# Splitting the normed mixer outputs where they are made, and passing them through DRAM as halves

## The chip, the cores and the metric

The kernel runs on one core of a Trainium2 chip. A core has five engines that run side by side, each with its own queue of instructions in a fixed order: TensorE (PE, matrix products), VectorE (DVE), ScalarE (ACT), GpSimd (POOL) and SyncE (SP, which here only issues DMA transfers). They share one on-chip memory (SBUF, 128 partitions) and the accumulators of TensorE (PSUM); DRAM is reached by DMA. The metric is the device time of one execution in microseconds.

## The reference

One layer of a decoder trunk over 2048 tokens of width 1024, in float32:

```python
proj = x @ w_in                       # q, k, v | b_gate, c_gate, h | p
mix  = concat(stick_breaking_attention(q, k, v),     # 8 heads x 64
              b_gate * conv3(c_gate * h),            # 4 groups x 64
              pooled(p) @ pool_w * pool_scale)       # 4 groups x 64
mix  = head_group_rmsnorm(mix, mix_norm_g)           # over each 64 columns
x = layer_norm(alpha * x + mix @ w_o, ln1_g, ln1_b)
x = layer_norm(alpha * x + relu(x @ w_up)**2 @ w_down, ln2_g, ln2_b)
```

## The kernel before

The tokens are cut into four chunks of 512. Products run on operands that are split into two halves: a tile t becomes hi = t rounded to the type that TensorE reads at full rate (fp32r), and lo = t - hi. A product of two such operands is then three products, hi by hi, hi by lo and lo by hi (lines 235 to 237 for the projections, 521 to 523 for the output). The helper `load` (line 177) makes the halves of what comes from DRAM: a DMA into a raw buffer (four buffers with the tag "raw", for all that is loaded this way), a cast on ScalarE (line 182), and a subtraction (line 184) on the engine that `low_engine` names: a counter of all such subtractions sends, from the fortieth on, every third to VectorE and the others to GpSimd.

The stages, by chunk pairs (0, 1) and (2, 3): projections of q, k and v, which go through DRAM already split; attention, which takes 224 of its 320 units in the second pair; the projections with convolution and pooling (`bchp`, groups 9, 7, 8 and 6 of the weights, for each pair); and the output stage (`out_stage`), which multiplies the normed mixer outputs by w_o, adds x, applies LayerNorm and sends the transposed rows on to the feed-forward part. From there on (classes `Up` and `down`) TensorE has products without a gap.

The order of instructions on each engine is set by a planner. It takes them by priority and by when a simulated machine could start them: blocks marked `early()` come first, attention (`PRIO`) second, and what bears no mark comes last, in the order of the program. So the unmarked projections, convolutions and output products fill in where attention leaves an engine free.

A mixer output of 128 columns of the concatenation (attention: the pair of heads j = 0 to 3; convolution j = 4, 5; pooling j = 6, 7) is normed by `rms` (line 281). A Square on ScalarE writes the tile `sq`. `rest` sums it by small products on TensorE, forms the inverse root (`rsqrt`, with a power on GpSimd), and spreads it into `sq` again. `scaled` transposes `sq` into PSUM and multiplies: `o = m * gain * ps` (line 302). Attention has one `sq` buffer and one `o` buffer ("a"). Convolution and pooling have one `sq` buffer for each of b0 and b1 and two buffers for `o`; the same buffers later hold LayerNorm's gain and bias (lines 559, 560). `sink` then does one thing: it stores `o` in DRAM, as `mscr[c][j]` (line 286).

`load_mix` (line 506) brings the eight outputs of a chunk back by `load`, at the highest priority, into the eight buffers of the tags "wh" and "wl". These are the buffers of the chunk before, and come free one by one as the last output product of that chunk reads them; the raw loads can run up to four tiles ahead. The last output of chunk 3 never leaves the chip: `last_mix` splits it in place of the store, on ScalarE and VectorE.

For chunk 0 the first products take four of its tiles first, and for chunk 3 seven of them (`ready`). The output product of a row block needs an accumulator in one of two PSUM buffers ("dn"), which line 554 on VectorE empties.

Of the kernel before, what the change touches and what calls it, by code (L numbers as in the profile page):

```python
# [10 lines left out]
F = mybir.dt.float32  # L11
R = mybir.dt.float32r
AF = mybir.ActivationFunctionType
ALU = mybir.AluOpType
# [3 lines left out]
P = 128  # L18
# [3 lines left out]
CH = 512  # L22
NC = S // CH
HEADS = 8
HD = 64
ND = D // P
# [17 lines left out]
def build(nc, tc, ctx, A, out):  # L44
    const = ctx.enter_context(tc.tile_pool(name="const", bufs=1))
    dram = ctx.enter_context(tc.tile_pool(name="dram", bufs=1, space=DRAM))

    nc.scalar.preload_act_table_set("sigmoid_and_others")
    ident = const.tile([P, P], F, name="ident")
    make_identity(nc, ident)  # L50
    eps_ln = const.tile([P, 1], F, name="eps_ln")
    nc.vector.memset(eps_ln, LN_EPS)

    qscr = [[dram.tile([2, HD, CH], F, name=f"qscr{c}_{h}") for h in range(HEADS)] for c in range(NC)]
    kscr = [[dram.tile([2, HD, CH], F, name=f"kscr{c}_{h}") for h in range(HEADS)] for c in range(NC)]
    vscr = [[dram.tile([4, P, 4, P], F, name=f"vscr{c}_{g}") for g in range(2)] for c in range(NC)]
    mscr = [[dram.tile([P, CH], F, name=f"mscr{c}_{j}") for j in range(ND)] for c in range(NC)]
    x1scr = [[dram.tile([P, D], F, name=f"x1scr{c}_{t}") for t in range(4)] for c in range(NC)]
    tscr = [[dram.tile([P, 2, 4, NQ, P], F, name=f"tscr{h}_{k}") for k in range(7)] for h in range(2)]
    hscr = [[[dram.tile([P, 4, CH], F, name=f"hscr{g}_{h}_{j}") for j in range(2)] for h in range(2)]  # L60
            for g in range(DFF // CH)]

    def split(dst_hi, dst_lo, src, scale=None):
        if scale is None:
            nc.scalar.copy(dst_hi, src)
            nc.vector.tensor_tensor(dst_lo, src, dst_hi.bitcast(F), ALU.subtract)  # L66
        else:
            nc.scalar.activation(dst_hi, src, AF.Identity, scale=scale)
            nc.vector.scalar_tensor_tensor(dst_lo, src, scale, dst_hi.bitcast(F), ALU.mult, ALU.subtract)

    expo = const.tile([P, 8], F, name="expo")
    nc.vector.memset(expo, -0.5)

    def rsqrt(pool, var, eps, shape, tag):

        v, s, t = (pool.tile(shape, F, name=f"{tag}{k}", tag=f"{tag}{k}", bufs=2) for k in "vst")
        nc.vector.tensor_scalar(v, var, eps, None, ALU.add)
        nc.gpsimd.tensor_tensor(s, v, expo[:, 0:shape[1]], ALU.pow)
        if shape[1] == 1:
            nc.vector.tensor_scalar(t, s, v, -0.5, ALU.mult, ALU.mult)  # L80
            nc.vector.tensor_scalar(t, t, s, 1.5, ALU.mult, ALU.add)
            nc.vector.tensor_scalar(s, s, t, None, ALU.mult)
            return s
        nc.vector.scalar_tensor_tensor(t, s, -0.5, v, ALU.mult, ALU.mult)
        nc.vector.scalar_tensor_tensor(t, t, 0.0, s, ALU.add, ALU.mult)
        nc.vector.scalar_tensor_tensor(s, t, 1.5, s, ALU.add, ALU.mult)
        return s

    def ln_stats(p, t, inverse):
        st = p.tile([P, 2, 6], F, name="st", tag="st", bufs=2)  # L90
        for i in range(2):
            nc.vector.bn_stats(st[:, i, :], t[:, i * 512:(i + 1) * 512])
        mv = p.tile([P, 2], F, name="mv", tag="mv", bufs=2)
        nc.vector.bn_aggr(mv, st)
        return mv[:, 0:1], inverse(p, mv[:, 1:2])

    def inverse_dve(p, var):
        return rsqrt(p, var, LN_EPS, [P, 1], "ln")

    def inverse_act(p, var):  # L100
        y, t = (p.tile([P, 1], F, name=f"ln{k}", tag=f"ln{k}", bufs=2) for k in "yt")
        nc.scalar.activation(y, var, AF.Ln, bias=eps_ln)
        nc.scalar.activation(y, y, AF.Exp, scale=-0.5)
        nc.scalar.activation(t, y, AF.Square)
        nc.vector.tensor_scalar(t, var, LN_EPS, t, ALU.add, ALU.mult)
        nc.vector.tensor_scalar(t, t, -0.5, 1.5, ALU.mult, ALU.add)
        nc.vector.tensor_scalar(y, y, t, None, ALU.mult)
        return y

    def layer_norm(p, t, g, b):  # L110
        m, y0 = ln_stats(p, t, inverse_dve)
        for i in range(2):
            h = t[:, i * 512:(i + 1) * 512]
            nc.vector.scalar_tensor_tensor(h, h, m, g[i], ALU.subtract, ALU.mult)
            nc.vector.scalar_tensor_tensor(h, h, y0, b[i], ALU.mult, ALU.add)

    def bcast(p, name):
        t = p.tile([P, D], F, name=name)
        nc.sync.dma_start(t, A[name].partition_broadcast(P))
        return t  # L120

    scr = qscr, kscr, vscr, mscr, x1scr, tscr
    with ExitStack() as up:
        pools = phase1(nc, tc, ctx, up, A, ident, scr, hscr, split, rsqrt, layer_norm, bcast)
    down(nc, tc, ctx, A, pools, hscr, x1scr, lambda p, t: ln_stats(p, t, inverse_act), bcast, out)


def phase1(nc, tc, whole, ctx, A, ident, scr, hscr, split, rsqrt, layer_norm, bcast):
    qscr, kscr, vscr, mscr, x1scr, tscr = scr
# [6 lines left out]
    pm = mixw.enter_context(tc.tile_pool(name="mixw", bufs=1, side="right", reuse_waits="tile"))  # L136
# [20 lines left out]
    for i in range(2):  # L157
        w = pd.tile([P, P], F, name=f"pw{i}")
# [18 lines left out]
    def load(src, name, shape, bufs):  # L177
        pool = px if name == "x" else pm
        raw = pd.tile(shape, F, name=f"{name}raw", tag="raw", bufs=RAW)
        nc.sync.dma_start(raw, src)  # L180
        h = pool.tile(shape, R, name=f"{name}h", tag=f"{name}h", bufs=bufs)
        nc.scalar.copy(h, raw)
        l = pool.tile(shape, R, name=f"{name}l", tag=f"{name}l", bufs=bufs)
        low_engine().tensor_tensor(l, raw, h.bitcast(F), ALU.subtract)
        return h, l
# [95 lines left out]
    def rms(m, j, c, ps_of, who):  # L281
        pool = p if who == "a" else pd
        sq = pool.tile([P, CH], F, name=f"sq{who}")
        nc.scalar.activation(sq, m, AF.Square)

        def rest(then, sink=lambda y: nc.sync.dma_start(mscr[c][j], y)):
            with early():
                var = ps_of()
                for t in range(4):
                    nc.tensor.matmul(var[:, 2 * t:2 * t + 2], sq[:, t * P:(t + 1) * P], blk, start=True, stop=True)  # L290
                y = rsqrt(pool, var[:, 0:8], RMS_EPS, [P, 8], f"rms{who[0]}")
                wide = sq.rearrange("p (g e) -> p g e", g=8)
                nc.scalar.activation(wide, y.unsqueeze(2).to_broadcast([P, 8, HD]), AF.Copy)

            def scaled():
                with early():
                    ps = ps_of()
                    for t in range(4):
                        ts = slice(t * P, (t + 1) * P)
                        nc.tensor.transpose(out=ps[:, ts], in_=sq[:, ts], identity=ident)  # L300
                    o = pool.tile([P, CH], F, name=f"o{who}", tag=f"rms{who[0]}y", bufs=len(who))
                    nc.vector.scalar_tensor_tensor(o, m, gain[:, j:j + 1], ps, ALU.mult, ALU.mult)
                    sink(o)
            then(scaled)
        return rest
# [190 lines left out]
    def halves(name, tags, bufs=1):  # L496
        t = []
        for i, tag in enumerate(tags):
            h = pd.tile([P, CH], F, name=f"{name}_{i}", tag=tag, bufs=bufs)
            nc.sync.dma_start(h, A[name][i * CH:(i + 1) * CH].partition_broadcast(P))  # L500
            t.append(h)
        return t

    mix = {}

    def load_mix(c, part):
        with early():
            mix.setdefault(c, []).extend(load(mscr[c][e], "w", [P, CH], ND) for e in part)

    def last_mix(y):  # L510
        h = pm.tile([P, CH], R, name="mh", tag="wh", bufs=ND)
# [157 lines left out]
class Up:  # L669
# [35 lines left out]
    def rest(self):  # L705
        self.pr = self.pool("upr")
        for i in (5, 6):
            self.load(0, i)
        pp = self.pt = self.whole.enter_context(self.tc.tile_pool(name="turnps", bufs=1, space=PSUM, side="right",
                                                                  reuse_waits="tile"))  # L710
        self.turn = Turn(self.nc, self.tc, self.pr, self.ident, self.tscr,
                         lambda: pp.tile([P, CH], F, name="tp", tag="tp", bufs=2),
                         {n: n for n in ("b0", "b1", "c0")} | {"x1h": "xs", "x1l": "xs"}, 3, nullcontext)
# [254 lines left out]
```

## Time and profile before

| | |
|---|---|
| median of 3 runs | 2456.9 us (2456.46 to 2458.3) |
| the profiled execution | 2459.65 us, span 2457.9 us |
| mean granted clock of TensorE | 0.994 |
| busy share of PE, DVE, ACT, POOL | 98%, 65%, 41%, 46% |
| instructions | 33072 |

The span is the time from the first to the last instruction of the profiled execution, which is what the rows below divide; its own time beside it includes what lies around the span. A busy share is an average over stages that differ. In views of windows each engine's column is its busy time in that stretch, PEclk the clock that TensorE was granted, as a share of full speed, and the DMA share the mean busy share of the 16 DMA engines.

### The profile page before, as it was taken

The page shows a single profiled execution, that of the slowest core. Times are in us where ns is not written, and L with a number is a line of the kernel's source. Part 1 is how long each engine was busy: PE and PEld are TensorE (multiplying, and loading weights), DVE is VectorE, ACT ScalarE, POOL GpSimd, SP SyncE. Part 2 cuts the span into 40 slices and gives each one's busy share as a digit, 9 for nine tenths or more (in the row PEclk, how much of TensorE's full clock was granted, in tenths as well). Part 3 has the DMA queues.
Part 4 walks back from the last instruction along what each step waited for, and adds up shares of the span by engine and source line. Part 5 has one row for each costly group of instructions (what it writes and reads, how often), then busy time and mean ns, then how long its engine had stood idle before and what let it go on. Part 6 is the DMA issues. An engine that isn't in the chain of part 4 may idle for free.

```text
span 2457.9 us, 33072 instructions
## 1 busy us (share of the span) xinstructions
PE 2398.0 (98%) x11728; PEld 1992.8 (81%) x11728; DVE 1589.8 (65%) x2227; ACT 1008.2 (41%) x1945; POOL 1136.3 (46%) x833
## 2 busy tenths in 40 slices
PE   8999999999999999999999999999999999999997
PEld 6988888778778787788888888888888888888886
DVE  3778777788987899976666656556316433333367
ACT  4667666655666656522333223222332101111123
POOL 2557555864775757634556545555201101101137
PEclk9999999999999999999999999999999999999999
DMA  8758645622422446557665383333525312212212
GB/s 239 193 148 235 174 138 148 195 78 91 158 82 95 141 149 220 201 216 289 221 225 192 112 333 125 116 103 112 173 75 172 110 53 86 86 49 78 80 60 112
DMA packets 164854, 360.37 MB, mean 147 GB/s; under 512 B 18640, under 2 KB 35024, under 8 KB 162896
## 3 DMA queue, kind: packets, MB, share of 16 engines
q1 hardware_dynamic: 164688, 358.25, 45.2%
q8 instruction: 93, 1.52, 0.3%
q14 instruction: 73, 0.60, 0.1%
HBM read 245.19 MB, written 112.98 MB: 146 GB/s over the span
## 4 chain that ended last, share of the span: by engine, by line
PE 78%; DVE 9%; DMA 4%; POOL 4%; issue 3%; ACT 2%; SPq 1%; DVEq 0%; ACTq 0%; POOLq 0%
PE dn L895 9%; PE dn L894 9%; PE dn L893 9%; PE b L792 7%; PE c L792 4%; PE a L792 4%; PE z L433 4%; PE dn L235 3%; PE dn L236 3%; PE b L795 3%; PE dn L237 3%; PE tp L465 3%; PE c L795 2%; PE a L795 2%; PE dn L521 2%
## 5 line engine op out<-in xcount | busy, mean ns | idle before, releaser
L448 POOL TENSOR_TENSOR g<-g,sig 128x512 f32<-128x512 f32 (+2 forms) x320 | 381.6, 1197 | 338.3 <-DVE g L446 144.4
L893 PE MATMUL dn<-d,ht 128*128 128x512 f32 x1024 | 398.3, 389 | 0.0
L894 PE MATMUL dn<-d,ht 128*128 128x512 f32 x1024 | 398.3, 389 | 0.0
L895 PE MATMUL dn<-d,ht 128*128 128x512 f32 x1024 | 397.7, 389 | 0.0
L732 POOL TENSOR_TENSOR w<-raw,w 128x512 fp32r<-128x512 f32 x186 | 253.9, 1371 | 240.9 <-ACT w L731 240.9
L899 DVE TENSOR_TENSOR y<-dn,y 128x512 f32<-128x512 f32 x224 | 154.2, 689 | 322.2 <-PE dn L895 322.1
L858 POOL TENSOR_TENSOR d<-draw,d 128x1024 fp32r<-128x1024 f32 x32 | 77.6, 2438 | 507.4 <-ACT d L857 507.2
L446 DVE TENSOR_TENSOR_SCAN g<-beta,g,z 128x513 f32<-128x513 f32 x192 | 244.1, 1275 | 48.5 <-ACT sig L438 46.3
L436 ACT ACTIVATE beta<-z 128x512 f32<-128x512 f32 (+2 forms) x320 | 172.9, 541 | 159.4 <-PE z L433 146.3
L871 ACT CAST ht<-draw 128x512 fp32r<-128x512 f32 x128 | 74.5, 620 | 380.3 <-PE dn L895 347.3
L895 PEld LDWEIGHTS dn<-d,ht 128*128 128x128 f32 x1024 | 192.2, 188 | 39.9
L893 PEld LDWEIGHTS dn<-d,ht 128*128 128x128 f32 x1024 | 192.2, 188 | 39.9
L894 PEld LDWEIGHTS dn<-d,ht 128*128 128x128 f32 x1024 | 192.2, 188 | 39.9
L731 ACT CAST w<-raw 128x512 fp32r<-128x512 f32 x186 | 114.1, 621 | 252.9 <-PE b L795 143.8
L235 PE MATMUL dn<-xh,wh 128*128 128x512 f32 x512 | 206.9, 407 | 10.3 <-DVE qk L66 5.3
L433 PE MATMUL z<-k,q 128*128 128x512 f32 (+3 forms) x640 | 192.6, 380 | 17.8 <-DVE g L446 12.7
L236 PE MATMUL dn<-xl,wh 128*128 128x512 f32 x512 | 206.8, 404 | 0.0
L237 PE MATMUL dn<-xh,wl 128*128 128x512 f32 x512 | 206.7, 404 | 0.0
L469 DVE TENSOR_TENSOR tl<-tp,th 128x512 fp32r<-128x512 f32 (+1 forms) x320 | 184.3, 596 | 30.3 <-ACT th L468 29.5
L465 PE MATMUL tp<-ident,g 128*128 128x128 f32 x1088 | 190.8, 274 | 1.9 <-DVE tl L469 0.8
L792 PE MATMUL b<-x,w 128*128 128x512 f32 x768 | 190.2, 390 | 2.1 <-ACT w L731 1.5
L468 ACT CAST th<-tp 128x512 fp32r<-128x512 f32 (+1 forms) x320 | 161.5, 535 | 63.9 <-PE tp L465 51.9
(195 smaller groups left out, 4983.9 us busy)
## 6 DMA issues: line engine op xcount, KB each, us to landing
hscr<-h SPq DMA_DIRECT2D x128, 256.0 KB, 2.8
draw<-hscr SPq DMA_DIRECT2D x64, 512.0 KB, 3.9
raw<-in_w_up SPq DMA_DIRECT2D x62, 512.0 KB, 4.4
x<-tscr SPq DMA_DIRECT2D x14, 2048.0 KB, 12.3
wraw<-in_w_in SPq DMA_DIRECT2D x80, 256.0 KB, 3.3
k<-kscr SPq DMA_DIRECT2D x80, 256.0 KB, 3.0
v<-vscr SPq DMA_DIRECT2D x80, 256.0 KB, 2.8
xraw<-in_xt SPq DMA_DIRECT2D x64, 256.0 KB, 3.1
```

The costliest lines, as they stand in the source:

```text
L235: nc.tensor.matmul(ps, wh, xh, start=(d == 0), stop=False)
L236: nc.tensor.matmul(ps, wh, xl, start=False, stop=False)
L237: nc.tensor.matmul(ps, wl, xh, start=False, stop=(d == ND - 1))
L433: nc.tensor.matmul(z[:, 0:w], q[:, b, j * P:(j + 1) * P], m["k"][:, 0:w], start=(b == 0), stop=(b == 1))
L446: nc.vector.tensor_tensor_scan(left, rev, idle, st["prev"][j][:, OFF - 1:OFF], ALU.mult, ALU.bypass)
L448: nc.gpsimd.tensor_tensor(gv, gv, sig[:, 0:w], ALU.mult)
L465: nc.tensor.transpose(out=tp[:, j * P:(j + 1) * P], in_=m["g"][j][:, cols], identity=ident)
L732: self.nc.gpsimd.tensor_tensor(w[:, 1], src, w.bitcast(F)[:, 0], ALU.subtract)
L792: nc.tensor.matmul(ps, wk[:, 0, d], x[:, i, :, d, :], start=(first and d == 0 and i == 0), stop=False, skip_group_check=True)
L893: nc.tensor.matmul(ps, hh[:, ts], dh[:, ds], start=(i == 0), stop=False)
L894: nc.tensor.matmul(ps, hh[:, ts], dl[:, ds], start=False, stop=False)
L895: nc.tensor.matmul(ps, hl[:, ts], dh[:, ds], start=False, stop=(i == 3))
```

## The change

The output `o` is split where it is made. The new function `halves` (not to be confused with the loader of the same name below it, line 496) casts `o` into the buffer of `sq`, which has been read by then, subtracts on GpSimd in place, and stores both tiles; the buffer in DRAM has room for the two. For convolution and pooling it runs outside the `early()` block, so with the priority of the program's unmarked parts; for attention with attention's own. The last output of chunk 3 keeps its way through `last_mix`. `load_mix` loads the two halves straight into "wh" and "wl", without a raw buffer, a cast or a subtraction.

```diff
-    mscr = [[dram.tile([P, CH], F, name=f"mscr{c}_{j}") for j in range(ND)] for c in range(NC)]
+    mscr = [[dram.tile([2, P, CH], F, name=f"mscr{c}_{j}") for j in range(ND)] for c in range(NC)]
...
-        def rest(then, sink=lambda y: nc.sync.dma_start(mscr[c][j], y)):
+        def halves(y):
+            hi, lo = sq.bitcast(R), y.bitcast(R)
+            nc.scalar.copy(hi, y)
+            nc.gpsimd.tensor_tensor(lo, y, sq, ALU.subtract)
+            nc.sync.dma_start(mscr[c][j][0], sq)
+            nc.sync.dma_start(mscr[c][j][1], y)
+
+        def rest(then, sink=halves):
...
                     nc.vector.scalar_tensor_tensor(o, m, gain[:, j:j + 1], ps, ALU.mult, ALU.mult)
+                    if sink is not halves:
+                        sink(o)
+                if sink is halves:
                     sink(o)
...
-            mix.setdefault(c, []).extend(load(mscr[c][e], "w", [P, CH], ND) for e in part)
+            for e in part:
+                t = [pm.tile([P, CH], F, name=f"w{n}", tag=f"w{n}", bufs=ND) for n in "hl"]
+                for i in range(2):
+                    nc.sync.dma_start(t[i], mscr[c][e][i])
+                mix.setdefault(c, []).append([a.bitcast(R) for a in t])
```

## Rows read from the trace of the kernel before

**Rows 1.** The page's first part: busy us (share of span) xinstructions, by engine.
```profile
PE 2398.0 (98%) x11728; PEld 1992.8 (81%) x11728; DVE 1589.8 (65%) x2227; ACT 1008.2 (41%) x1945; POOL 1136.3 (46%) x833
```
**Rows 2.** Windows: stretch, length, busy of PE, PEld, DVE, ACT, POOL, PEclk, DMA share, GB/s.
```profile
100.00:440.00 340.00, 336.77 (x2046) 294.89 (x2045) 261.98 (x359) 225.27 (x484) 192.93 (x162) 1.00 0.60 166
500.00:850.00 350.00, 334.33 (x1736) 269.89 (x1735) 295.78 (x408) 217.45 (x441) 230.96 (x179) 0.99 0.34 107
850.00:1130.00 280.00, 268.61 (x1335) 219.29 (x1333) 244.98 (x387) 132.04 (x259) 151.13 (x118) 0.99 0.57 196
...
1600.00:1650.00 50.00, 50.00 (x223) 41.39 (x222) 30.76 (x37) 14.05 (x24) 27.68 (x20) 1.00 0.35 114
```
**Rows 3.** The same view, two stretches of 10 us in the output stage.
```profile
850.00:860.00 10.00, 7.93 (x31) 6.15 (x29) 9.21 (x13) 8.46 (x17) 9.24 (x8) 0.83 0.63 201
940.00:950.00 10.00, 7.09 (x32) 5.36 (x33) 9.81 (x13) 8.50 (x17) 10.00 (x8) 1.00 0.74 240
```
**Rows 4.** Groups by line and form, 820 to 1140: count, busy us, mean ns, idle before.
```profile
L184 POOL TENSOR_TENSOR wl<-wraw,wh 128x512 fp32r<-128x512 f32 x21 | 30.1, 1443 | 6.1 <-PE dn L522 3.7 <-ACT wh L182 2.4
...
L182 ACT CAST wh<-wraw 128x512 fp32r<-128x512 f32 x31 | 18.6, 631 | 27.1 <-PE dn L522 16.5 <-DMA wraw<-mscr 10.2
...
L184 DVE TENSOR_TENSOR wl<-wraw,wh 128x512 fp32r<-128x512 f32 x10 | 10.8, 1077 | 4.6 <-ACT wh L182 4.1 <-PE dn L522 0.4
```
**Rows 5.** Timeline of PE: start, duration, instruction, [idle before it <-releaser].
```profile
853.32 1.22 PE L433 MATMUL z<-k,q 128*128 128x512 f32 x2 [2.07 <-DVE rmsbt L85]
...
941.22 0.73 PE L433 MATMUL z<-k,q 128*128 128x512 f32 x2 [1.27 <-DVE g L446]
...
946.01 0.50 PE L521 MATMUL dn<-xh,wh 128*128 128x512 f32 x1 [1.69 <-DVE r L554]
...
1031.52 0.65 PE L650 MATMUL dn<-ident,r 128*128 128x128 f32 x4 [1.28 <-DVE x1l L628]
```
**Rows 6.** Timeline of DVE, three subtractions of mixer tiles.
```profile
938.84 1.13 DVE L184 TENSOR_TENSOR wl<-wraw,wh 128x512 fp32r<-128x512 f32 x1
...
943.76 1.60 DVE L184 TENSOR_TENSOR wl<-wraw,wh 128x512 fp32r<-128x512 f32 x1
...
1029.01 0.67 DVE L184 TENSOR_TENSOR wl<-wraw,wh 128x512 fp32r<-128x512 f32 x1
```
**Rows 7.** The chain of waits from 845 to 853 us: start, us, what.
```profile
847.97 1.25 POOL wl L184
849.21 1.61 POOL rmsbs L78
```
**Rows 8.** Mixer buffer: stores (ns min/median/max, first to last), DMA median us to landing.
```profile
L286 SPq DMA_DIRECT2D mscr<-ob x16: 319/323/383, 533.0 to 886.3; - x16
L286 SPq DMA_DIRECT2D mscr<-oa x15: 319/327/540, 117.2 to 983.1; - x15
...
wraw<-mscr SPq DMA_DIRECT2D x31, 256.0 KB, 2.9
...
mscr<-ob SPq DMA_DIRECT2D x16, 256.0 KB, 2.2
```
**Rows 9.** Timeline of DVE, two outputs of the first pooling round.
```profile
532.19 0.74 DVE L302 SCALAR_TENSOR_TENSOR ob<-pl,gain,dn 128x512 f32<-128x512 f32 x1
...
545.46 0.71 DVE L302 SCALAR_TENSOR_TENSOR ob<-pl,gain,dn 128x512 f32<-128x512 f32 x1
```
**Rows 10.** Timeline of ACT, the Squares of the next two pooling outputs.
```profile
533.02 0.65 ACT L284 ACTIVATE sqb<-pl 128x512 f32<-128x512 f32 x1
...
543.83 0.69 ACT L284 ACTIVATE sqb<-pl 128x512 f32<-128x512 f32 x1
```
**Rows 11.** Windows of PE between two dense products: stretch, length, busy, PEclk, DMA, GB/s.
```profile
520.25:532.98 12.73, 9.14 (x41) 1.00 0.15 42
722.25:733.95 11.70, 10.33 (x53) 1.00 0.26 90
```
**Rows 12.** Timeline of ACT at the boundary into chunk 3.
```profile
1078.76 1.30 ACT L182 CAST wh<-wraw 128x512 fp32r<-128x512 f32 x2 [16.53 <-PE dn L522]
```

## The prediction

> **What bounds the kernel now.** I read the page first: TensorE (PE) is busy 2398.0 of 2457.9 us [rows 1], so at most some 60 us can be won by anything that leaves PE's work as it is, and this change leaves it so. Next the busy time by stage. From 1150 us on PE is fed: one 50 us stretch there shows 223 products in 50.00 busy us [rows 2], and 50 / 223 = 0.224 us is what one 128x512 product takes when nothing stops it. Nothing that this change touches runs in that part. What can move is ahead of it, where attention (high priority) and the dense stages (low priority, as fillers) share PE: of 100 to 440 us PE lacks 3.2 us, of 500 to 850 us 15.7 us, of 850 to 1130 us, the output stage, 11.4 us [rows 2]. The reader is to see that PE's idle time in these stretches is the whole purse: 4.5% of 500 to 850 and 4.1% of 850 to 1130.
>
> Then the 10 us slices in which PE is worst off. At 850 to 860 and 940 to 950 PE has 2.07 and 2.91 us idle, while VectorE (DVE) is at 9.2 and 9.8, GpSimd (POOL) at 9.2 and 10.0 and ScalarE (ACT) at 8.5 of 10 [rows 3]. These are the moments in which one chunk's mixer outputs are loaded and split: 31 casts on ACT (18.6 us), 21 subtractions on POOL (30.1 us) and 10 on DVE (10.8 us) [rows 4], in bunches of seven or eight.
>
> **Part 1, what is removed.** The timeline of PE names who ended its gaps: 1.69 us before the first product of chunk 1 at 946.01, by the eviction at line 554; 1.27 us at 941.22, by a scan; 1.28 us at 1031.52, by DVE; 2.07 us at 853.32, by a small rms instruction on DVE [rows 5]. On DVE, subtractions of line 184 stand directly ahead: 1.60 us at 943.76 ahead of the eviction, 1.13 us at 938.84 ahead of the scan that frees PE at 941.22, 0.67 us at 1029.01 [rows 6]. Without them the releases come earlier by 1.6, 1.1 and 0.6: 3.3 us. At 853.32 the chain goes through POOL: a mixer subtraction of 1.25 us at 847.97, then the power of the rms chain at 849.21 [rows 7]; without it 1.25 us. The same slice has its granted clock at 0.83 where 940 to 950 has 1.00 [rows 3]; that is 1.7 us of PE. The slice at 940 has more idle time and no such fall, so the gap alone does not explain it, and I count half, 0.85. Sum of the gains: 3.3 + 1.25 + 0.85 = 5.4 us. From below the gain is 0, if another wait stands behind each one taken away; from above it is all of the idle time of 850 to 1130 and the clock, 11.4 + 1.7 = 13.1. I take 5.4, because each piece is a row that stands directly ahead of a gap. The last output-weight loads also share the counter that sends every third subtraction to DVE; eight fewer ahead of them shifts which ones, by one subtraction at most, and I price that at nothing.
>
> **Part 2, what is added where the outputs are made.** Each of 31 outputs gets a cast on ACT (0.63 us by the 31 casts today), a subtraction on POOL (1.44 by the 21), and a second 256 KB store behind the first on SP's queue. Fifteen belong to attention (from 117.2 us) and sixteen to convolution and pooling (533.0 to 886.3) [rows 4, 8]. By the stores' times nine fall before 440 us, where PE lacks only 3.2 of 340 us: hidden under PE. Seventeen fall into 500 to 850, 17 x 1.44 = 24.5 us more on POOL, whose products attention waits for. POOL is busy 231 of 350 us there [rows 2], so it has room; I price each added us with PE's share of idle time there, 4.5%, 1.1 us, between 0 and 28% (the worst share, below), 6.9. The other five fall into 850 to 983, where POOL loses more than it gets.
>
> The other cost is a buffer. The high half is written over the tile sq, which has one buffer for each of b0 and b1 and for attention. Today sq is free after its transposes; afterwards it is free only when the cast, the subtraction and the first store are through. The next Square waits for that. The row to look at is the pooling round: the output at 532.19 ends at 532.93 and the next Square follows at 533.02; the second output at 545.46 ends at 546.17, and its Square had begun at 543.83 [rows 9, 10]. After the output come 0.63 for the cast and 2.2 for the store [rows 8], 2.8 us, with the subtraction beside the store. So the Squares go back by 2.8 - 0.1 = 2.7 and 2.8 + 2.3 = 5.1, about 4 us. Behind a Square stand the rms chain, the output, and so the buffer into which the next dense product is copied: the dense stream stops longer by about as much. While it stood still at 520 to 533 PE was idle for 3.59 of 12.73 us (28%), in the second round for 1.37 of 11.70 (12%) [rows 11]. So the price is 4 x (0.28 + 0.12) = 1.6 us; 0 if attention fills the gap, and 2 x 10 x 0.28 = 5.6 if the low priority lets each split wait some 6 us for attention's instructions.
>
> Attention's own sq is asked for again only a head pair later, (983.1 - 117.2) / 14 = 62 us on average by its fifteen stores [rows 8], so it costs nothing there. LayerNorm's gain and bias take over the b buffers, about 3 us later; the three buffers of its rows cover that, and without them it would cost those 3 us once.
>
> **Part 3, what the loads become.** A mixer load was 256 KB into a raw buffer, four of them ahead of time; now it is two loads of 256 KB straight into the operands' buffers, which come free only as the last product of the chunk before reads them. Per chunk 16 transfers instead of 8, and none ahead of time. At 940 to 950 the DMA engines moved 240 GB/s at 0.74 busy [rows 3], 324 GB/s when full. The boundary without attention is that into chunk 3: the first free buffer shows as the cast at 1078.76, for which ACT had stood 16.53 us until PE released it [rows 12]. Seven pairs are 3.67 MB, 11.3 us; the first lands after 2.9 [rows 8], of which its own transfer is 0.8, so the last lands at 1078.7 + 2.1 + 11.3 = 1092.1. PE frees the buffers with 3 products of 0.224 us each, so the first product of chunk 3 starts 7 x 0.67 = 4.7 us after the first release, at 1083.4, and wants its seventh pair at 1087.4: 4.7 us too early, if products run one by one. Two accumulators are open at that time, and 14 triples take 9.4 us, so with both products advancing as tiles land the last pair is wanted at 1083.4 + 9.4 - 1.3 = 1091.5, and 0.6 us is lost. Two row loads of 512 KB (line 544) that get ahead in the queue add 3.2 us. I take 1.5, between 0 and 4.7 + 3.2 = 7.9. At the two other boundaries attention has work for PE meanwhile; I take 0, and 4.7 x 0.28 = 1.3 each from above.
>
> **Sum:** -5.4 + 1.1 + 1.6 + 1.5 = -1.2 us. The profiled execution took 2459.65 us with a span of 2457.9; the median of the runs is 2456.9, 0.1% lower. Taken from the median: 2455.7.
>
> **Rivals.**
> Faster: VectorE sets the pace of the output stage (245 of 280 us, and 9.8 of 10 in the worst slice [rows 2, 3]), and the 10.8 us of subtractions come back whole, with no loss at the boundaries: -10.8 + 1.1 + 1.6 = -8.1, so 2448.8. For it: four gaps end on DVE. Against it: PE has only 11.4 us idle there, and one of the gaps belongs to POOL.
>
> Slower: the halves land late. No load runs ahead, so at the boundary into chunk 3 the full 7.9 is lost, at the two others 1.3 each, and the 3.3 us of relief at these are not seen: -5.4 + 3.3 + 1.1 + 1.6 + 10.5 = +11.1, so 2468.0. It decides from the point at which the last pair lands 5 us or more after PE wants it. For it: the 11.3 us of transfers against 9.4 us of products. Against it: two accumulators, and three engines that no longer stand between the load and the product.
>
> Slower by the buffer: both pooling rounds pay 10 us of stopped dense work, twice each: 4 x 10 x 0.28 = 11.2 in place of 1.6, so +8.4 and 2465.3. Against it: POOL and ACT have gaps of some us at 533.
>
> POOL becomes late in 500 to 850: 6.9 in place of 1.1, so +4.6 and 2461.5. POOL takes 1.44 us for what DVE does in 1.08 [rows 4], and all 31 go to POOL. The Trainium skill, "GPSIMD Engine Reference", section 4.1 (Engine selection), says that two-input elementwise work belongs on VectorE, since GpSimd is about 2 times slower: it speaks against the placing, and by it alone the sum would be the one just given. The trace bears out the direction, with a factor of 1.3 rather than 2.
>
> **How the numbers follow.** A measurement of this kernel can tell about 0.2%, 4.9 us. Forecast 0.35, POOL late 0.06: within 0.2%, 0.41. Relief comes back whole 0.36: faster. Halves late 0.16, buffer 0.07: slower, 0.23. The forecast's own range, with a piece of relief more or a boundary less, is 2451 to 2461. The range that leaves out about one in ten on each side goes from 2446 (the faster case with one more gap closed) to 2466 (most of the late halves).
>
> **What would show it.** Right: at 850, 940 and 1030 us DVE and POOL below 9 of 10 and PE's gaps shorter; no line 182 or 184 on mixer tiles; 62 loads and 62 stores of 256 KB; Squares of the second pooling outputs some 4 us after the outputs before them; the first products of chunk 3 spread out by tile landings, no more than 2 us idle. Wrong: PE gaps in front of the output products that end on a DMA from the mixer buffers; the dense stream standing still for 20 us or more in the pooling rounds; or PE idle in 850 to 1130 falling to under 4 us.

## The result and the profile after

The changed kernel takes 2471.68 us (median of 4 runs, 2470.57 to 2474.31), the kernel before, run beside it, 2457.6 (2456.46 to 2458.3): ratio 1.0061, 95% interval 1.0049 to 1.0074. It is slower by 14.1 us, which lies outside the range of the prediction and on the other side of its forecast. The profiled execution of the changed kernel took 2474.31 us with a span of 2472.5.

The page's first part and the windows of three stretches after the change, which answer to [rows 1, 2] (stretch, length, busy of PE, PEld, DVE, ACT, POOL, PEclk, DMA share, GB/s):

```profile
PE 2409.3 (97%) x11728; PEld 2000.2 (81%) x11728; DVE 1590.0 (64%) x2217; ACT 1003.8 (41%) x1945; POOL 1145.6 (46%) x843
```
```profile
100.00:440.00 340.00, 334.63 (x2023) 292.87 (x2022) 263.83 (x353) 225.45 (x486) 201.93 (x167) 0.99 0.61 171
500.00:850.00 350.00, 332.24 (x1684) 268.01 (x1685) 294.77 (x401) 219.29 (x447) 244.47 (x191) 0.97 0.39 118
850.00:1130.00 280.00, 268.90 (x1334) 218.32 (x1334) 234.97 (x377) 125.17 (x248) 138.00 (x109) 0.98 0.66 228
```

The reader is to see three things. The work on PE is the same: 11,728 products in both. POOL has 9 us more in all, DVE the same, but PE takes 11.3 us more for its same products. And the stretch of 500 to 850 is where PE gets less done: 1,684 products against 1,736 [rows 2], at a granted clock of 0.97 against 0.99, while it is busy for only 2.1 us less.

So PE's busy time grew although its work did not; the clock says why. Where TensorE stood in the changed kernel and what its clock did then, first the gaps (timeline of PE), then the windows around them:

```profile
520.89 0.50 PE L235 MATMUL dn<-xh,wh 128*128 128x512 f32 x1 [3.25 <-ACT pa L349]
...
676.17 1.22 PE L443 MATMUL z<-k,q 128*128 128x512 f32 x2 [2.94 <-ACT sig L448]
...
740.90 0.48 PE L480 MATMUL o<-th,v 128*128 128x128 f32 x1 [2.16 <-ACT th L478]
...
897.18 0.55 PE L481 MATMUL o<-tl,v 128*128 128x512 f32 x1 [2.29 <-DVE tl L479]
```
```profile
518.00:526.00 8.00, 5.11 (x18) 4.16 (x18) 5.86 (x10) 4.45 (x10) 5.97 (x6) 0.79 0.43 138
...
676.00:684.00 8.00, 7.83 (x29) 6.49 (x30) 7.34 (x11) 6.10 (x14) 7.03 (x6) 0.60 0.60 199
...
738.00:748.00 10.00, 7.16 (x25) 5.04 (x25) 7.89 (x9) 5.13 (x11) 6.55 (x5) 0.66 0.13 41
896.00:905.00 9.00, 5.75 (x16) 4.01 (x17) 8.30 (x17) 6.01 (x12) 4.83 (x5) 0.58 0.42 132
```

Each of these four gaps is followed by a stretch in which the clock falls from 2.4 to 1.2 GHz and PE does its products at half speed; not every gap is (one of 1.99 us at 635.04 in the kernel before was not). None of the four ends on a split: they end on the copy of a dense product, on attention's sigmoid and on attention's halves. One step further back ACT had stood for the last VectorE step of an rms chain (line 86) in three of them (timeline of ACT):

```profile
519.73 0.63 ACT L300 ACTIVATE sqb<-rmsbs 128x512 f32<-128x512 f32 x1 [3.92 <-DVE rmsbs L86]
...
673.91 0.63 ACT L300 ACTIVATE sqb<-rmsbs 128x512 f32<-128x512 f32 x1 [1.93 <-DVE rmsbs L86]
...
739.58 0.63 ACT L300 ACTIVATE sqb<-rmsbs 128x512 f32<-128x512 f32 x1 [2.54 <-DVE rmsbs L86]
```

In the second of these a split does take part: its subtraction on GpSimd runs beside that step (rows in the last section). Added up from the trace's records, ahead of the last product the clock stood at 1.2 GHz for 41.0 us in 8 stretches after the change, for 17.1 us in 3 before it; PE stood idle for 45.4 us against 42.6. At half speed half the time is lost: (41.0 - 17.1) / 2 = 11.9, and 2.8 more idle make 14.7, against the 14.2 us by which the last product of the profiled execution is later. The same account holds within about 4 us for every kernel in the table at the end of the experiments.

### The profile page after: what moved, and what is told of

The parts are those of the page before. It is cut to its first block, busy times and chain, and to the rows that moved or that the text cites. A ratio compares the mean times of both kernels' runs of the same rounds, so it can differ in the third digit from the quotient of the medians.

```text
span 2472.5 us, 33210 instructions
## 1 busy us (share of the span) xinstructions
PE 2409.3 (97%) x11728; PEld 2000.2 (81%) x11728; DVE 1590.0 (64%) x2217; ACT 1003.8 (41%) x1945; POOL 1145.6 (46%) x843
## 4 chain that ended last, share of the span: by engine, by line
PE 78%; DVE 9%; DMA 4%; POOL 3%; issue 3%; ACT 2%; SPq 1%; DVEq 0%; ACTq 0%; POOLq 0%
PE dn L908 9%; PE dn L907 9%; PE dn L909 9%; PE b L806 7%; PE c L806 4%; PE a L806 4%; PE z L443 4%; PE b L809 3%; PE tp L475 3%; PE dn L235 3%; PE dn L236 3%; PE dn L237 3%; PE c L809 2%; PE dn L535 2%; PE a L809 2%
```

## The experiments

Four theories stood at the start. Queue: the low-priority casts and subtractions hold up what stands behind them on ACT and GpSimd. Buffer: the Square waits for its tile. GpSimd: its 31 subtractions are late or slow VectorE. Plan: the operations cost little, and the loss is the new order that the planner writes for every engine once anything in the program is another. The fourth got its decisive runs last.

**Parts of the change.** The high half in a buffer of its own, out of the raw loads' pool:
```
-            hi, lo = sq.bitcast(R), y.bitcast(R)
-            nc.scalar.copy(hi, y)
+            t = pd.tile([P, CH], R, name=f"hi{who}", tag="raw", bufs=RAW)
+            nc.scalar.copy(t, y)
```


> The high half goes into a raw buffer of its own instead of over sq, so sq is free after its transposes as in the kernel before; cast, subtraction, stores and loads stay as in the changed kernel. Buffer theory (the next Square waits for cast, subtraction and store, and the dense stream behind it stands still): the stops at the Squares go, 2452 to 2460 us. Queue theory (the cast stands in ScalarE's fixed order ahead of attention's sigmoids and waits there for VectorE's output): no change, 2467 to 2474 us. Plan theory (any edit gives the planner another order, and the loss is that order's luck): anywhere from 2450 to 2475.

2654.91 us, ratio 1.081 (1.0785 to 1.0834). It tells nothing of the Square's tile: by 1105 us TensorE is 193 us late, a stall that covers everything else. That the splits, at the lowest priority, hold raw buffers that the dense loads want is the likely reason, not a shown one.

No split at all (e2); the output is stored into both halves as it is:
```
+            for i in range(2):
+                nc.sync.dma_start(mscr[c][j][i], y)
```


> No cast and no subtraction: the unsplit output is stored into both halves and both are loaded, so the numbers of the output stage are not the reference's. Stores, loads and their bytes are those of the changed kernel. Buffer theory and queue theory alike: sq is free early and ScalarE's queue has no cast, so the loss upstream goes and the gain of the output stage (its products from the third on took 239.8 us instead of 245.6) stays, 2448 to 2455 us. If the second store and the doubled loads are the loss: 2468 to 2474.

2461.33, ratio 1.0012 (1.0003 to 1.0022). All the relief and none of the splits, and yet nothing is won: the first sign that the relief is not to be had by itself. (By its trace TensorE's order is another one here too, from about 666 us on.)

Splits made, but the loader loads the high half and splits it again (e3):
```
-                t = [pm.tile([P, CH], F, name=f"w{n}", tag=f"w{n}", bufs=ND) for n in "hl"]
...
+            mix.setdefault(c, []).extend(load(mscr[c][e][0], "w", [P, CH], ND) for e in part)
```


> The splits are made and stored as in the changed kernel, but the loads are those of the kernel before: the high half alone through the raw buffer, cast and subtraction (so the low half is zero and the result is that of the rounded operand). Buffer and queue theory: the loss upstream without the gain of the output stage, 2474 to 2482 us. If the loads are the loss: 2455 to 2460.

2478.78, ratio 1.0082 (1.0063 to 1.0100). The making alone seems to cost 21 us.

The kernel before, with the counter that picks the subtractions' engine set back by eight ahead of the last output weights (e4):
```
     load_mix(0, EORDER)
+    count[0] -= 8
     load_wo(EORDER[4:])
```


> The kernel before, with the counter of the low halves set back by eight ahead of the last output-weight loads, as the change does by loading eight fewer: only which of eight subtractions run on VectorE differs. All theories but the plan theory: 2455 to 2460 us. Plan theory: off by up to 10 us either way.

2462.89, ratio 1.0025 (1.0014 to 1.0036). In the trace nothing is lost up to 957 us; from 1000 us on, where the shift also moves later chunks' subtractions to the other engine, 5 us are. TensorE's order parts from that of before at 854 us.

**Queue, buffer, subtraction, and half of the outputs.** The cast on VectorE, right behind the output:
```
+                    if sink is halves:
+                        nc.vector.tensor_copy(sq.bitcast(R), o)
...
-            nc.scalar.copy(hi, y)
```


> The cast of the high half is taken from ScalarE and put on VectorE, directly behind the output that it casts and at the same high priority; all else is as in the changed kernel, with sq still held until the subtraction and the store are through. Queue theory: ScalarE no longer stands for the casts (24.0 us in 14 waits in the changed kernel), so half or more of the loss upstream goes, 2457 to 2465 us. Buffer theory: the Squares still wait, 2467 to 2473. VectorE's own 31 casts, some 0.5 us each, may cost 2 to 5 us of it.

2468.95, ratio 1.0042 (1.0027 to 1.0057): 3 us less than the changed kernel. The queue theory wanted half of the loss or more; and as the order is another one again, even these 3 us are not a price of the cast's place on ACT.

The high half of the dense outputs in a buffer that is idle then, so that the Square's tile is free early:
```
+            t = sq if who == "a" else pd.tile([P, 2, CH], F, name="hib", tag="big", bufs=3)[:, 0]
+            nc.scalar.copy(t.bitcast(R), y)
```


> For convolution and pooling the high half goes into a buffer that is idle at that time (the three of the projections' outputs and the output stage's rows) instead of over sq; for attention all is as in the changed kernel. Cast and subtraction stay on ScalarE and GpSimd. Buffer theory: the Squares of the pooling rounds follow the outputs as before and the dense stream stops no longer than before, 2458 to 2465 us. Queue theory: 2467 to 2473.

2475.9, ratio 1.0064 (1.0043 to 1.0084). The buffer theory falls.

The change without the subtraction (the low half is stored unsplit):
```
-            nc.gpsimd.tensor_tensor(lo, y, sq, ALU.subtract)
```


> The changed kernel without the subtraction on GpSimd: the second half stored is the unsplit output, so the output stage's numbers are not the reference's. ScalarE's casts and the hold on sq until its store stay. If GpSimd's 31 subtractions (and the slower VectorE beside them) are the loss: 2457 to 2463 us. Queue and buffer theory: 2465 to 2472.

2455.02, ratio 0.9990 (0.9981 to 1.0000). The loss is gone with the subtractions, and by a little more than any theory forecast. At this point the GpSimd theory led.

Only the 16 outputs of convolution and pooling split where they are made:
```
+            sink = sink or (halves if j >= 4 else lambda y: nc.sync.dma_start(mscr[c][j][0], y))
```


> Only the sixteen outputs of convolution and pooling are split where they are made; attention's fifteen are stored whole and split by the loader as in the kernel before. Buffer theory: nearly all of the loss stays, since the Squares that wait are these sixteen, 2466 to 2473 us. Queue theory: the waits of ScalarE for attention's casts (18.1 of 24.0 us) go, 2459 to 2465.

2465.46, ratio 1.0024 (1.0015 to 1.0034). This lies between the ranges of the two theories and decides nothing.

**The GpSimd theory tried.** The subtraction on VectorE:
```
-            nc.gpsimd.tensor_tensor(lo, y, sq, ALU.subtract)
+            nc.vector.tensor_tensor(lo, y, sq, ALU.subtract)
```


> The changed kernel with the subtraction of each split on VectorE in place of GpSimd; the cast, the second store, the holding of the Square's buffer and the loading of halves stay. If the 31 subtractions cost through GpSimd (its fixed order, or VectorE's short instructions slowed while it runs), the time stands between 2453 and 2460 us: what the kernel without subtractions gave (2455.0) plus at most 31 x 0.6 us of VectorE, mostly covered. If any subtraction between the output and its store costs the same wherever it stands, it stays within 4 us of the changed kernel's 2471.7.

2474.44, ratio 1.0070 (1.0057 to 1.0083). As slow as on GpSimd. So it is not GpSimd's speed or its order. The Trainium skill, "GPSIMD Engine Reference", section 4.1 (Engine selection), which the prediction weighed, says that GpSimd is about 2 times slower at two-input elementwise work. The durations agree (medians of the split's subtraction: 1.30 us on GpSimd in the changed kernel, 0.69 on VectorE here); yet by that rule alone this run should have won some of the loss back, and it did not.

GpSimd's subtractions alone, added to the kernel before and used by nobody (e14):
```
+        def halves(y):
+            nc.sync.dma_start(mscr[c][j], y)
+            nc.gpsimd.tensor_tensor(sq, y, y, ALU.subtract)
```


> The kernel before, with one GpSimd subtraction of 128x512 added behind each of the 31 stores at the lowest priority, written into the Square's buffer and used by nobody; no cast, one store, the loader splits as before. It prices GpSimd's subtractions by themselves. GpSimd theory: about +15 to +20 us over the kernel before (2473 to 2478), with the product's milestones of 458 to 513 us and 656 to 711 us falling behind as in the changed kernel. If the loss needs the cast or the second store as well: within 5 us of 2457.9.

2478.77, ratio 1.0088 (1.0074 to 1.0102). The total fits the GpSimd theory, the place does not. Its windows of 440 to 860 us, and under it the kernel before:

```profile
440.00:860.00 420.00, 396.24 (x2069) 320.34 (x2067) 358.31 (x479) 263.51 (x533) 307.62 (x238) 0.98 0.38 116
```
```profile
440.00:860.00 420.00, 397.33 (x2061) 320.99 (x2060) 351.74 (x480) 264.87 (x534) 288.41 (x223) 0.98 0.39 120
```

GpSimd does 19.2 us more in this stretch, and PE gets 2,069 products done against 2,061. By the table below nothing is lost up to 859 us, though 26 of the 31 have started by then; the whole loss comes behind it.

Only the eight attention outputs of chunks 0 and 1 split where they are made:
```
+            sink = sink or (halves if (j < 4 and c < 2) else lambda y: nc.sync.dma_start(mscr[c][j][0], y))
```


> The changed kernel with the split where it is made for the attention outputs of chunks 0 and 1 alone (8 of 31); the others go through DRAM whole and are split by the loader as before. GpSimd theory: these 8 subtractions fall in 100 to about 500 us, where TensorE stood little, so the loss before the output stage is 0 to 4 us; the relief is at most that of chunk 0's and 1's loads, so 2453 to 2460. If the mere regrouping of the loads costs as much as the subtractions, it is over 2462.

2472.89, ratio 1.0058 (1.0045 to 1.0071). Eight splits, the last at 364 us, cost what 31 do, and most of it shows long after they are through: in its trace 2.1 us at 365 us, 8.9 at the end.

The splits with the output's own high priority:
```
-                    if sink is not halves:
-                        sink(o)
-                if sink is halves:
-                    sink(o)
+                    sink(o)
```


> The changed kernel with the splits at the same high priority as the output itself, so each subtraction goes into GpSimd's order right behind its output and not later. If the loss comes from where the lowest priority puts the subtractions in GpSimd's order (among multiplies of attention that are due), it falls to 2455 to 2465; if it comes from GpSimd's time as such, it stays near 2471.7 or above.

2470.77, ratio 1.0055 (1.0040 to 1.0070). The lowest priority is not the cause either. By itself this leaves GpSimd's time as such standing; against that speak the subtraction on VectorE, and the places of the loss in e14 and with eight splits.

**The order tried by itself.** The instructions as the planner wrote them for TensorE in the two kernels, at the first place where they part, number 622 of 11,594, around 122 us, just behind the first attention output's split (z are attention's scores, dn dense products):
```
before                              after
dn<-xh,wh                           dn<-xh,wh
dn<-xl,wh                           dn<-xl,wh
z<-k,q                              dn<-xh,wl
z<-k,q                              dn<-xh,wh
dn<-xh,wl                           dn<-xl,wh
dn<-xh,wh                           z<-k,q
dn<-xl,wh                           z<-k,q
```
From there the two lists drift apart. The traces, which hold 11,728 records, bear it out: with each product named by its tiles, buffer numbers left out, the two kernels are the same for 625 records, then differ at 3,759 places up to the 6,011th, and attention's 1,500th product (scores, transposes and outputs together) stands 48 places earlier after. So the change gives TensorE another program, not the old one with 31 splits more. To see what another order is worth, one ACT copy of a single column (0.19 us) goes in ahead of one attention Square, in the kernel before and in the changed one, ahead of the first (j = 0) or the third (j = 2):
```
+        if c == 0 and j == 0:
+            nc.scalar.copy(sq[:, 0:1], m[:, 0:1])
         nc.scalar.activation(sq, m, AF.Square)
```


> The kernel before with one more ACT copy, of a single column of 128 values, ahead of the first attention output's Square; no split is moved. Its work is some 0.2 us, but the planner writes TensorE another order from about 104 us on. Theory of cost: 2456 to 2460, as before. Theory of order: anywhere in 2450 to 2478, with milestones in 450 to 900 us that part from those of before by 5 us or more.

2471.82, ratio 1.0055 (1.0042 to 1.0067).

> The same single-column copy in the kernel before, ahead of the third attention output's Square: TensorE's written order parts from that of before at about 225 us. Theory of cost: 2456 to 2460. Theory of order: anywhere in 2450 to 2478; of the two made from the kernel before at least one lies over 2463 or under 2453.

2468.66, ratio 1.0042 (1.0029 to 1.0055).

> The changed kernel with the same single-column copy ahead of the first attention output's Square: all 31 splits where they were made, but another written order from about 104 us on. Theory of cost: 2469 to 2476, as the changed kernel. Theory of order: anywhere in 2448 to 2478; at least one of the two made from the changed kernel lies under 2465.

2471.14, ratio 1.0054 (1.0040 to 1.0068).

> The changed kernel with the single-column copy ahead of the third attention output's Square: TensorE's written order parts from that of the changed kernel at about 225 us. Theory of cost: 2469 to 2476. Theory of order: anywhere in 2448 to 2478.

2476.43, ratio 1.0079 (1.0065 to 1.0093).

A fifth of a microsecond of work makes the kernel before 14.4 and 11.3 us slower, as much as the change does. In one point the theory of order missed: neither of the two made from the changed kernel came under 2465. The control: the same copy ahead of the fourth attention Square (j = 3), where the written orders of TensorE, VectorE, GpSimd and SyncE stay those of before. The traces agree: these four engines' instructions stand in the same order, and on ACT the Square alone comes two places later, behind two of attention's.

> The kernel before with the single-column ACT copy ahead of the fourth attention output's Square, a place at which the written orders of TensorE, VectorE, GpSimd and SyncE stay those of the kernel before and ACT's has this one instruction more. Theory of order: 2456 to 2460, no change. If the copy itself costs the 11 to 14 us that it cost at the other two places: 2468 to 2472.

2457.43, ratio 0.9999 (0.9990 to 1.0008). So it is not the copy, but what the planner makes of it. The copy took 0.19 us at 229.8 us with j = 2 and 0.22 us at 249.3 us with j = 3. Three windows of each of these two kernels, j = 2 first:

```profile
871.00:879.00 8.00, 6.10 (x22) 4.69 (x21) 6.71 (x9) 3.46 (x9) 5.12 (x5) 0.79 0.85 238
889.00:897.00 8.00, 7.36 (x27) 5.76 (x28) 8.00 (x15) 2.19 (x5) 4.01 (x3) 0.79 0.56 192
1039.00:1047.00 8.00, 6.84 (x26) 5.40 (x26) 7.21 (x14) 4.08 (x9) 5.02 (x4) 0.79 0.83 271
```
```profile
871.00:879.00 8.00, 7.06 (x48) 5.88 (x47) 7.96 (x19) 6.35 (x15) 4.84 (x6) 1.00 0.63 188
889.00:897.00 8.00, 8.00 (x47) 6.90 (x46) 6.71 (x11) 4.97 (x11) 3.26 (x3) 1.00 0.36 126
1039.00:1047.00 8.00, 7.91 (x41) 6.26 (x40) 5.55 (x10) 3.46 (x7) 1.29 (x1) 1.00 0.19 72
```

The two kernels hold the same instructions. Their sources differ only in where one copy stands, and by that in the planner's order; 640 us later the one has gaps and a clock at 0.79 where the other has less idle time and its full clock. The gaps of the first end on a step of attention, a small step of the rms chain and the eviction of an output product (timeline of PE):

```profile
873.97 1.01 PE L435 MATMUL z<-k,q 128*128 128x384 f32 x2 [0.92 <-DVE g L448]
...
889.42 0.73 PE L435 MATMUL z<-k,q 128*128 128x512 f32 x2 [1.75 <-DVE rmsbs L86]
...
1038.84 0.66 PE L652 MATMUL dn<-ident,r 128*128 128x128 f32 x4 [1.89 <-DVE r L556]
```

Last, splits with TensorE's order kept: six outputs for which its written order differs from that of before at 253 of its 11,594 places, 250 of them in the output stage. Their loads are those of the changed kernel, the other outputs' those of the kernel before; this part of the edit is left out here, as it is above for the 16 and the 8 splits.
```
+            sink = sink or (halves if (c, j) in ((3, 0), (3, 1), (3, 2), (2, 0), (1, 0), (1, 2))
+                            else lambda y: nc.sync.dma_start(mscr[c][j][0], y))
```


> The changed kernel with the split where it is made for six outputs alone (chunk 1's first and third, chunk 2's first, chunk 3's first three), chosen because TensorE's written order then differs from that of before at only 253 of its 11,594 places; the other 25 go whole and are split by the loader. Theory of order: 2453 to 2460. If splits at the place of making cost as 8 of them did in 117 to 365 us (14.7 us, 1.8 each): about 2468.

2458.44, ratio 0.9997 (0.9988 to 1.0006). Six splits cost nothing that can be measured, where eight others cost 14.7 us with another order; at that price six would have cost 11. The other 25 were not tried with the order kept.

The table, from TensorE's records in the traces: by how many us TensorE starts its instruction number N later than in the kernel before, the time PE stood idle, and the time at 1.2 GHz ahead of the last product. "From" is the place in TensorE's written order (11,594 places) from which it is another one; N counts the trace's 11,728 records.
```
                       from   N=2966  4600   5800  11700   idle  1.2 GHz
before                         523us   859   1105   2439   42.6   17.1
after                   622     +9.3  +8.1  +14.5  +14.2   45.4   41.0
splits early (e7)       622     +7.6  +5.6   +9.1  +10.7   45.2   30.7
other buffer (e10)      622     +3.8  +5.8  +14.8  +15.7   47.5   34.1
subtract on DVE (e13)   622     +8.4  +6.1  +15.1  +14.3   48.5   37.5
cast on DVE (e6)        617     +8.1  -1.3   +4.6   +5.8   46.5   27.3
after, copy j=0 (e17)   522    +10.2  +3.2  +17.8  +18.3   53.4   37.5
after, copy j=2 (e22)   622     +6.0  +2.3  +14.9  +15.7   49.7   34.1
8 splits (e15)          622     +7.2  +3.3   +9.8   +8.9   44.4   34.1
16 splits (e9)         2966     -2.6  -5.8   +0.5   +0.9   40.7   30.7
no subtraction (e12)    622     +2.9  -5.1   -4.0   -4.2   38.7   17.1
subtraction only (e14) 2879     -0.7  -0.1  +16.7  +18.5   50.8   41.0
before, copy j=0 (e5)   522     +3.8  -3.3   +9.5   +9.2   47.2   27.3
before, copy j=2 (e21) 1278     +0.8  -6.6   +8.0   +9.4   48.6   27.3
before, copy j=3 (e23) kept     -3.4  -4.6   -5.1   -5.4   39.1   17.1
6 splits (e24)        (2465)    -0.9  +0.8   +0.9   +0.1   37.0   34.1
```
These are single profiled executions, so differences of up to about 5 us mean nothing: the control stands at -5.4 here with a median equal to that of before. In the last row the order is another one at 253 places only.

## Why the prediction was wrong

**The step that failed is the sum.** It adds the prices of what is removed, added and moved to a time in which everything else keeps its place. It does not: the planner places every later instruction anew. This term is missing in the sum and among the rivals, and it is the largest: two edits of 0.2 us cost 11.3 and 14.4 us. The prediction touches it once, at the counter that picks the subtractions' engine, and prices it "at nothing"; the shift of that counter by itself (e4), which gives another order from 854 us on, measured 5.0 us. The order of the kernel before is the better one: no kernel with the whole work whose order parts for good from it within the first 3,000 places came under 2465 us. Measured against those two, the change looks cheap: the seven kernels of the table with all 31 splits stand at 1.0042 to 1.0079, on average 1.0061, the two bare copies at 1.0049 on average; the difference is 0.0012, 3 us, and with two orders on one side it can't be told from the -1.2 of the sum, nor from 0. So whether the parts of the sum add up to about nothing is not shown; that another order by itself costs as much as the change did is. The faster rival, all subtractions coming back (2448.8), did not come either.

**PE fed from 1150 us on: right.** The delay is 14.6 us at 1152 and 14.2 at the end.

**Part 1, the relief (5.4 us): seen, but not the change's own.** From the output stage's third accumulated product (each is of 24 single ones) to its last PE stood idle for 8.2 us before and 4.1 after, but over the whole stretch of 850 to 1130 for 11.4 and 11.1. Ahead of an output product one gap of over 1 us is left (timeline of PE), smaller than that of [rows 5]:

```profile
1065.68 0.50 PE L535 MATMUL dn<-xh,wh 128*128 128x512 f32 x1 [1.20 <-DVE b L651]
```

But with the same loads and another order (e17, e22) the 4.1 us were 8.0 and 9.3, and with the bare copies ahead of j = 0 and 2 the 8.2 were 8.8 and 8.7. A row directly ahead of a gap tells who ended it in this order; another order has its gaps elsewhere. That is the premise of Part 1 that did not hold. (Its three rows add to 3.4, not 3.3.) Of the signs that it named, GpSimd fell below 9 of 10 in all three slices (5.9, 5.9 and 7.0); VectorE did so at 850 alone (7.2, then 9.2 and 10.0).

**Part 2, GpSimd (1.1 us, bound 6.9): not contradicted.** 19 us more of it in 440 to 860 show no loss for TensorE up to 859 us (e14), and six splits with the order kept none at all (e24). This speaks against the rival "POOL becomes late", for which e12 alone spoke; but e14 has another order from 514 us on, and orders alone moved TensorE by up to 6.6 us at 859. The factor of 1.3 between the two engines that the prediction worked out compares means of a wide spread; by the shortest subtractions of weights and mixer tiles at line 184 in the kernel before (1.26 and 0.66 us) it is 1.9. **The buffer (1.6 us): the mechanism right, the wait longer, its price not shown.** The pooling round after, outputs on DVE and Squares on ACT, which answer to [rows 9, 10]:

```profile
539.87 0.75 DVE L309 SCALAR_TENSOR_TENSOR ob<-pl,gain,dn 128x512 f32<-128x512 f32 x1 [0.36 <-PE dn L307]
...
552.82 0.73 DVE L309 SCALAR_TENSOR_TENSOR ob<-pl,gain,dn 128x512 f32<-128x512 f32 x1
```
```profile
545.77 0.63 ACT L284 ACTIVATE sqb<-pl 128x512 f32<-128x512 f32 x1 [3.95 <-POOL ob L289]
558.03 0.61 ACT L284 ACTIVATE sqb<-pl 128x512 f32<-128x512 f32 x1
```

The Squares follow 5.2 and 4.5 us behind the outputs' ends (forecast: 2.8 each), the first one ended by the subtraction, not by the store: the sum had put the subtraction beside the store and left out its wait for GpSimd (the first stood there behind two of attention's multiplies, until 544.45). With the Squares' wait taken away (e10) the time did not fall, in another order again.

**Part 3, the halves' loads (1.5 us): right in kind and nearly in size.** The mixer buffers in the trace after (ns min/median/max, first to last), who waited for them (us, times), and the landing:

```profile
L521 SPq DMA_DIRECT2D wh<-mscr x31: 319/320/804, 814.2 to 1101.1; - x31
L521 SPq DMA_DIRECT2D wl<-mscr x31: 319/382/1605, 816.4 to 1101.7; - x31
...
  PEld dn L535: 1.6, 4
  PEld dn L537: 0.7, 2
  PE dn L535: 0.3, 1
...
DMA to landing us min/median/max: 2.0/3.9/6.9
```

The output products waited 2.6 us in all for halves; the rival "halves land late" (10.5 us) did not come.

**What stays open.** Which property of the order of before keeps its gaps short was not shown: only that gaps of 1 to 3 us, ended by attention's and the rms chain's steps, come in other places and take the granted clock down more often. One property goes with the loss in the traces. The 63 small VectorE steps of the rms chains (lines 84 to 86, 128x8 values) that start in 440 to 910 us take 35.6 us in all before and 33.6 to 35.7 in the kernels that lose about 5 us at most (e2, e4, e12, e23, e24), but 38.0 to 44.7 in the twelve other kernels of the table. They are long where GpSimd is at work beside them (last section), so an order that puts them there stretches the chains; that this makes the loss is not shown, and the longest sum (e6) does not have the greatest loss. Nor is it known why the change without subtractions (e12), which has a new order too, loses nothing; it may be the luck of its order or the missing work. No version that beats both kernels was found: 2455.02 (e12) leaves out work, and the six splits with the order kept (e24) are level.

## What to carry to other kernels

Where a planner writes the order of all engines, a small edit is a new program: before a per cent is put down to what an edit does, run an edit that does nothing, at two or three places, and see how far the time scatters. Then compare with the order kept, by choosing a place or a part at which the written order stays, since an experiment that undoes one part of a change gives yet another order and seems to point at that part, as the run without subtractions did. When TensorE's busy time grows with the same products, add up its extra idle time and half of its extra time at 1.2 GHz: here that gave the loss within about 4 us.

## What the runs showed of the hardware

Short gaps cost about as much again by the clock as by themselves, in all but two of the slower kernels (e17, e21) more: over the kernels of the table idle time differs from that of before by -5.6 to +10.8 us, time at 1.2 GHz by up to 23.9, of which half is lost.

A GpSimd subtraction of 128x512 in the splits took 1.30 us (median), the one of e14 1.04. Rows of after, and of e14:

```profile
L289 POOL TENSOR_TENSOR ob<-ob,sqb x16: 1255/1298/1758, 544.5 to 906.0; 128x512 fp32r<-128x512 f32 x16
```
```profile
L288 POOL TENSOR_TENSOR sqb<-ob x16: 1033/1040/1486, 532.2 to 900.9; 128x512 f32<-128x512 f32 x16
```

The type of the result does not make the difference: attention's multiplies of 128x512 write plain f32 and took 1.34 us on average in the changed kernel (line 458), as these subtractions did (1.35). What sets e14 apart is that it reads one tile as both inputs; that this is the reason was not tried.

A VectorE instruction of the rms chain on 128x8 values took from 0.11 to 1.26 us in the changed kernel. The long ones stand until a GpSimd instruction beside them is through: all 48 of its 96 steps (lines 84 to 86) that took over 0.3 us ended within 0.1 us of the end of one, and so did all 45 in the kernel before. Two pairs of the changed kernel, POOL and DVE, the second beside a split's subtraction:

```profile
517.89 1.38 POOL L184 TENSOR_TENSOR wl<-wraw,wh 128x512 fp32r<-128x512 f32 x1
518.13 1.15 DVE L85 SCALAR_TENSOR_TENSOR rmsbt<-rmsbt,rmsbs 128x8 f32<-128x8 f32 x1
...
672.59 1.25 POOL L289 TENSOR_TENSOR ob<-ob,sqb 128x512 fp32r<-128x512 f32 x1
672.69 1.19 DVE L86 SCALAR_TENSOR_TENSOR rmsbs<-rmsbt,rmsbs 128x8 f32<-128x8 f32 x1
```

The Trainium skill, "GPSIMD Engine Reference", section 8 (Key points), says that GpSimd shares its SBUF interfaces with VectorE's two-input instructions; these ends agree with it.
